# The output gate of a gated linear attention made by seven block products after the heads instead of eight tiles between them

## The chip, the core and the metric

The kernel runs on one core of a Trainium2 chip. The core has five engines with an instruction queue each: TensorE (PE in the profile) for matmuls, VectorE (DVE), ScalarE (ACT), GpSimd (POOL) and SyncE (SP), which here only issues transfers. POOL issues transfers too, and those it issues may add to what lies at their destination. The engines wait for each other by semaphores. What is measured is the time of one execution in microseconds (us); lower is better.

## The reference, cut to what matters

One layer of a decoder trunk, 512 tokens of 1024 channels in fp32:

```python
u = _rmsnorm(h, norm1_g[l])
proj = u @ w_in[l]
a_glu, q, k, v, r, g_low, gate_a, gate_b = _split_cols(proj)

c = a_glu[..., :CONV_CH] * jax.nn.sigmoid(a_glu[..., CONV_CH:])
c = _causal_dwconv(c, conv_dw_w[l], conv_dw_b[l])
c = jax.nn.silu(_layernorm(c, conv_ln_g[l], conv_ln_b[l]))
y_conv = c @ w_conv_out[l]
...
o = _gla_chunked(qh, kh, vh, gkh)
o = o * lax.rsqrt(jnp.mean(o * o, axis=-1, keepdims=True) + EPS) * gla_norm_g[l].astype(jnp.float32)
o = o.reshape(bsz, seq, GLA_VDIM).astype(x.dtype) * jax.nn.silu(r)
y_gla = o @ w_gla_out[l]

merged = jax.nn.sigmoid(gate_a) * y_conv + jax.nn.sigmoid(gate_b) * y_gla
h = h + merged @ w_o[l]
```

After this come an RMSNorm, a channel mixer of width 2816 with a short causal convolution, its residual, and the last RMSNorm. The change concerns r, a 512 x 1024 product of u with a 1024 x 1024 weight.

## The kernel before, in words

**Products in fp32.** Each fp32 operand is split into a high part in a short format and a low part, the rest. A product is three matmuls (`mm3`, lines 448 to 450: low by high, high by low, high by high). Activations are split once; weights are split as they come, in `split_weight`: the high part by an ACT copy (line 385, or 355 for the blocks of summed products), the low part by a DVE subtraction (390, 356). For tiles named in the set `ADDED` the low part is made without DVE: ACT writes the negated weight, rounded to the short format (387), and a transfer issued by POOL adds the weight from memory to it (388).

**A tile** of an ordinary projection is one weight tile of 128 x 1024 (128 output channels, eight blocks of 128 input channels), times all 512 tokens: 8 x 3 = 24 matmuls with 512 columns. The result has channels on partitions.

**Order.** The list `order` gives all weights in the order of use. `weight(...)` takes the next and splits those up to two ahead (`LOOK`), so that DVE, ACT and POOL prepare a weight while PE multiplies an earlier one. Loads are issued by SP in the same order, as buffers come free. Behind each weight, `fill` deals out a share of other DVE work: the taps of the depthwise convolution (`conv_chain`, line 788: 31 taps per channel tile, folded to 46 half-width operations and a few sums), and the list `urgent`. A scheduler arranges each engine's instructions by costs that it assumes, with the waits that follow; on the chip each engine runs its list strictly in order.

**Stages.** First half of v; eight pairs of GLU tiles, each of which starts a chain of taps; the low-rank gate; second half of v. Then four heads, one step apart: for a new head the decays, q (one tile), k (one tile), and for the head before it the scores (line 1031 transposes k), the states and the outputs. In each head stand two tiles of r (`gate_r`, line 1096: the product and silu). Behind the last head come four tiles of merge gate B. `gated` transposes o to channels on partitions (1085), multiplies by gain and silu of r (1088) and splits the result. Next, three tiles of w_gla, and the merge: six groups (`pair_7`, `MERGE`) in which two tiles are made by four block products, with halves of w_gla and w_conv tiles behind them (`BEHIND`). These need sums of token blocks of u, made by DVE as `urgent` work (`token_sums_7`, 1137), and their high and low parts (1145, 1150). The layer norm over the convolved channels runs beside this.

**Seven products.** w_o and w_down are multiplied by `seven`, a scheme in the manner of Strassen: both operands are seen as 2 x 2 blocks, and seven products of sums of blocks (`STEPS`: a11, a12, s1, n2, n3, s4, a22) replace eight. Each product is 24 matmuls of 128x512 for a matrix of this size. The sums of weight blocks are made by accumulating transfers (300, 317) and by DVE (310) in buffers called `kept`; results are added to the residual (1419).

Of the kernel before, what the change touches and what calls it, by code (L numbers as in the profile page):

```python
# [17 lines left out]
P = 128  # L18
D = 1024
T = 512  # L20
# [17 lines left out]
_HALVES = [("w_gla", 3 + h // 2, h % 2) for h in range(10)]  # L38
BEHIND = [_HALVES[:3], _HALVES[3:6], _HALVES[6:9], _HALVES[9:]]
# [4 lines left out]
ADDED = {("w_glu", 2 * k) for k in range(2, KT)} | {("w_r", m) for m in range(KT)}  # L44
ADDED |= {("w_v", KT // 2 + j) for j in (0, 1)}
# [6 lines left out]
SEVEN = {"w_o": KT // 2, "w_down": FT // 2}  # L52
# [23 lines left out]
def trunk_layer(ctx: ExitStack, tc: tile.TileContext, a: dict, out: bass.AP):  # L76
# [135 lines left out]
    order += [("w_glu", 2 * k + j) for k in range(KT) for j in (1, 0)]  # L212
    order += [("w_low", 0), ("w_low", 1)]
    order += [("w_v", KT // 2 + j) for j in range(KT // 2)]
    for h in range(HEADS):
        order += [("w_qk", 2 * h), ("w_qk", 2 * h + 1), ("w_r", 2 * h), ("w_r", 2 * h + 1)]
    order += [("w_gb", m) for m in range(AHEAD)] + [("w_gla", m) for m in range(AHEAD - 1)]
    tight = set()
    first = len(order)
    for (name, p, q), behind in zip(MERGE, BEHIND):  # L220
        for n, part in enumerate(("x1", "x3", "x2", "x4")):
            order.append(("two", (name, p, q, part)))
            order += [tile[:2] for tile in behind[n : n + 1] if tile[2] == 0]
    tight |= set(range(first, len(order)))
# [46 lines left out]
    def block(name, pairs, d, row, col):  # L271

        pairs = pairs[2 * d : 2 * d + 2]
        first = pairs[0][row]
        w = a[name][col * SEVEN[name] + first // 2]
        return w if len(pairs) == 2 else w[:, row * T : (row + 1) * T]

    def keep_tile(name):
        if name == "w_o":
            return tp.tile([P, D], F32, tag="x", name=nm("kept"), bufs=3)  # L280
        return fp.tile([P, D], F32, tag="kept", name=nm("kept"), bufs=2)

    LOADS = {"a11": (0, 0), "a12": (1, 0), "n2": (1, 1), "n3": (0, 1)}

    def load_block(name, pairs, step, d):
# [4 lines left out]
        n = src.shape[-1]  # L290
# [5 lines left out]
        load_dma = nc.sync.dma_start(dst, src)  # L296
        if name == "w_down":
            tc.keep_in_program_order(load_dma)
        if step == "n3":
            nc.gpsimd.dma_start(dst, block(name, pairs, d, 1, 1), accum_op=ALU.add)  # L300
# [12 lines left out]
    def sum_on(name, pairs, step, d):  # L313

        if step in ("a11", "n2"):
            nxt = block(name, pairs, d, *((0, 1) if step == "a11" else (1, 0)))
            nc.gpsimd.dma_start(kept[pairs, d], nxt, accum_op=ALU.add)
# [90 lines left out]
    def weight(name, j, ahead=LOOK):  # L408
# [4 lines left out]
        share = {"two": 2.5, "w_glu": RATE + 0.75}.get(name, RATE)  # L413
# [7 lines left out]
    after, urgent, hold = [], [], [True]  # L421
    behind = []

    def start_chain():
        if not chains and after and not (hold and len(after) == 1):
            chains.append(after.pop()())
# [389 lines left out]
    for k in range(KT):  # L816
        pg = col_tile(weight("w_glu", 2 * k + 1), acts1)
        sg = tmp()
        nc.scalar.activation(sg, pg, AF.Sigmoid)
        pa = col_tile(weight("w_glu", 2 * k), acts1)  # L820
        c = heap()
        nc.vector.tensor_tensor(parted(c), paired(pa), paired(sg), ALU.mult)
        chains.append(conv_chain(k, c))


    ca = [None] * KT
    stat = {}
# [54 lines left out]
    def ln_out(k):  # L882
# [6 lines left out]
        hi = late.tile([P, T], F32R, tag="ch", name=nm("ch"), bufs=KT)  # L889
# [91 lines left out]
    class Head:  # L981
# [79 lines left out]
        def outputs(self):  # L1061
            self.o = tp.tile([P, NT, DV], F32, tag="x", name=nm("o"), bufs=3)
# [15 lines left out]
            for p, half in enumerate(halves):  # L1078
                nc.scalar.activation(self.o[:, p, :], half, AF.Copy, scale=r[:, p : p + 1])

        def gated(self, last=False):
            for s in range(2):
                po = ax_bank() if s or last else mm_bank()
                for p in range(NT):
                    nc.tensor.transpose(po[:, p * P : (p + 1) * P], self.o[:, p, s * P : (s + 1) * P], ident)  # L1085
                f = tmp()
                m = 2 * self.h + s
                nc.vector.scalar_tensor_tensor(f, po, pp[:, PP_GG + s : PP_GG + s + 1], sr[m], ALU.mult, ALU.mult)
                oa[m] = split(f)

    sr = [None] * KT

    def gate_r(m):
        pr = col_tile(weight("w_r", m), acts1)
        sr[m] = heap()
        nc.scalar.activation(sr[m], pr, AF.Silu)
# [118 lines left out]
    def quarters(pool, tag, bufs, halves=1, dt=F32R):  # L1215
# [4 lines left out]
    x_src, x_room, gain_room = quarters(tp, "x", 3, dt=F32), quarters(tp, "x", 3), quarters(tp, "gain", 1)  # L1220
    b_src = quarters(tp, "tmp", 6, 2, F32)
    late_room = lambda: quarters(late, "sums", 3)()
# [3 lines left out]
        {"s1": x_src, "n2": x_src, "s4": b_src, "n3": b_src},  # L1226
        {"s1": c_room, "n2": x_room, "s4": late_room, "n3": late_room},
        {"s1": gain_room, "n2": x_room, "s4": late_room, "n3": x_room},
    )


    heads = [Head(h) for h in range(HEADS)]
    for h in range(HEADS + 1):
        old = heads[h - 1] if h else None
        new = heads[h] if h < HEADS else None
        if new:
            new.decays()
# [3 lines left out]
        if old:  # L1241
            old.scores(heads[h - 2].gated if h > 1 else None)
# [8 lines left out]
    behind += [roots_at[0], low_at[0]]  # L1251
    gla_scope.close()
    late_scope, late = scoped("late", 1, "right")


    s1_n2, of_s1, s4, of_n2, of_s4, n3, of_n3 = merge_sums
    while len(after) > 1:
        fill(1)
    hold.clear()
    start_chain()  # L1260
    chains[0].pop(0)[1]()
    urgent += s1_n2 + of_s1 + s4 + of_n2 + of_s4 + n3 + of_n3
# [28 lines left out]
    for m in range(AHEAD):  # L1291
        part[m] = sigmoid(m, gbs.pop(m))
        if m < AHEAD - 1:
            tile_of("w_gla", m, range(KT))
# [5 lines left out]
    def pair_7(n):  # L1300
        (name, p, q), behind = MERGE[n], BEHIND[n]
        unit = two_tiles(name, p, q, lambda: merge_acts, mm_bank, len(behind) < 3)
        if behind[0][0] == "w_conv":
# [22 lines left out]

    for n in range(4):
        pair_7(n)

# [37 lines left out]
    behind.clear()  # L1367
    late_scope.close()
    res_scope, rp = scoped("residual", 1, "right")
    ctx.push(res_scope)  # L1370


    def seven(name, pairs, acts, complete, at=lambda step, i: None, fine=False):

        bank = {"x": [mm_bank(), mm_bank()], "y": [mm_bank(), mm_bank()], "z": [ax_bank(), ax_bank()]}  # L1380
        of = {"a11": "x", "n2": "x", "n3": "x", "a22": "x", "s1": "y", "s4": "y", "a12": "z"}

        into = {
            "a11": (0, 0, ALU.add, False),
            "a12": (0, 0, ALU.add, True),
            "s1": (1, 1, ALU.add, False),
            "n2": (0, 1, ALU.subtract, False),
            "s4": (0, 1, ALU.add, True),
            "n3": (1, 1, ALU.subtract, True),
            "a22": (1, 0, ALU.add, True),  # L1390
        }

        def products(step, i, parts, acc, lo=0, hi=T, opens=False):
            acc = acc[:, lo:hi]
            opens = opens or step in ("a11", "s1", "a12")
            for d, w in parts:
                for j, pair in enumerate(acts[2 * d : 2 * d + 2]):
                    ah, al = (x[:, i * P : (i + 1) * P] for x in pair[step])
                    c = slice(j * T + lo, j * T + hi)

                    read = 2 * d + j == len(acts) - 1
                    mm3(acc, (ah, al), (w[0][:, c], w[1][:, c]), opens and d == 0 and j == 0, read, not opens)

        steps = list(STEPS)
        while steps:
            step, d = steps.pop(0)

            with tc.issue_after(freed.ins) if step == "a22" and not fine else ExitStack():
                parts = [(d, weight(name, (pairs, step, d)))]
                if steps and steps[0] == (step, 1):  # L1410
                    steps.pop(0)
                    parts.append((1, weight(name, (pairs, step, 1))))
            half, n, op, whole = into[step]
            for i in range(2):
                t = 2 * half + i
                acc = bank[of[step]][i]

                def add(n, acc, c=slice(0, T)):
                    done = nc.vector.tensor_tensor(hres[t, n][:, c], hres[t, n][:, c], acc[:, c], op)  # L1419
                    if whole:  # L1420
                        complete(t, n, c)
                    return done

                if fine and (step, i) == ("a22", 1):
                    products(step, i, parts, acc, 0, H)
                    rest = mm_bank()
                    products(step, i, parts, rest, H, T, True)
                    with tc.manual_schedule(engines={ET.DVE, ET.Activation}):
                        add(n, acc, slice(0, H))
                        add(n, rest, slice(H, T))  # L1430
                    continue
                products(step, i, parts, acc)
                if parts[-1][0] == 1:
                    at(step, i)
                    done = add(n, acc)
                    if (step, i) == ("n3", 1):
                        freed = done
                if fine and (step, i) == ("n3", 1):

# [339 lines left out]
```

## Time and profile before

| | |
|---|---|
| three runs | 821.64, 821.17, 821.0 us; median 821.17 |
| the profiled execution | 820.78 us, its span 818.9 us |
| PE busy | 810.3 us, 99% of the span |
| DVE busy | 715.6 us, 87% |
| ACT busy | 448.9 us, 55% |
| POOL busy | 148.8 us, 18% |
| granted clock of PE | 0.999 of full speed |

The span runs from the first to the last instruction. Busy time counts the instructions on an engine; a matmul's record overlaps with the next one's, so PE's busy time is not the sum of its records' lengths. In a row of groups stand line, engine, operation, output and input tiles, shape and count, then busy time, mean ns of one, and the idle time ahead with what ended it. A row of windows has the stretch, its length, and for PE, weight load, DVE, ACT and POOL the busy time and count, then the granted clock, the share of the 16 DMA engines and GB/s. The waits name who waited for whom: us in total, times, longest. A row of the timeline has start, duration and the instruction. A row of transfers has the count, KB each and the median time from issue to landing.

### The profile page before, as it was taken

The numbers are of one execution on the slowest core, as the hardware profiler recorded it, in microseconds if no ns is written. First come the engines' busy times: TensorE is split into PE (matmuls) and PEld (weight loads), VectorE is DVE, ScalarE is ACT, GpSimd is POOL, SyncE is SP. The second block draws the span as 40 slices with busy tenths as digits, with TensorE's granted clock in tenths as the row PEclk, the third lists the DMA queues.
The fourth block names the chain that finished last, engine by engine and source line by source line (L and its number), as shares of the span: only waits on it lengthen the run. The fifth ranks groups of instructions, "written<-read, shape, count | busy, mean of one in ns | idle before, by whom it ended". The sixth has DMA issues, their size and how long they took to land.

```text
span 818.9 us, 11480 instructions
## 1 busy us (share of the span) xinstructions
PE 810.3 (99%) x4287; PEld 700.5 (86%) x4287; DVE 715.6 (87%) x1157; ACT 448.9 (55%) x666; POOL 148.8 (18%) x133
## 2 busy tenths in 40 slices
PE   9999999999999999999999999999999999999996
PEld 7888888888888889999988898898889988899885
DVE  6689999999989699885788889979965999789896
ACT  6643447656663446684444556556435663466554
POOL 2000010001000213633001000230123301622012
PEclk9999999999999999999999999999999999999999
DMA  8355572563532123223657623146642447334662
GB/s 318 104 127 144 148 188 96 130 154 104 120 97 96 49 62 109 88 78 129 206 115 220 187 71 103 52 161 166 134 137 89 144 123 167 104 103 177 158 129 102
DMA packets 30615, 106.25 MB, mean 130 GB/s; under 512 B 3464, under 2 KB 3600, under 8 KB 30560
## 3 DMA queue, kind: packets, MB, share of 16 engines
q1 hardware_dynamic: 24784, 85.34, 30.4%
q0 software_dynamic: 5760, 20.19, 14.4%
q8 instruction: 33, 0.54, 0.3%
q14 instruction: 22, 0.18, 0.1%
q10 hardware_dynamic: 16, 0.00, 0.0%
HBM read 103.42 MB, written 2.10 MB: 129 GB/s over the span
## 4 chain that ended last, share of the span: by engine, by line
PE 98%; DMA 1%; ACT 0%; DVE 0%; POOL 0%; issue 0%; POOLq 0%; SPq 0%; ACTq 0%
PE mm L448 28%; PE mm L449 28%; PE mm L450 28%; PE mm L662 3%; PE ax L450 2%; PE ax L448 2%; PE ax L449 2%; PE ax L1070 1%; PE ax L1072 1%; PE ax L1051 1%; DMA raw<-in_w_v_dram 1%; PE ax L1040 0%; PE ax L529 0%; PE ax L576 0%; PE ax L1085 0%; PE mm L933 0%
## 5 line engine op out<-in xcount | busy, mean ns | idle before, releaser
L448 PE MATMUL mm<-uh,wlo 128*128 128x512 f32 (+1 forms) x672 | 244.4, 364 | 0.0
L449 PE MATMUL mm<-ul,whi 128*128 128x512 f32 (+1 forms) x672 | 242.4, 361 | 0.0
L450 PE MATMUL mm<-uh,whi 128*128 128x512 f32 (+1 forms) x672 | 242.0, 360 | 0.0
L450 PEld LDWEIGHTS mm<-uh,whi 128*128 128x128 f32 x672 | 126.8, 189 | 19.4
L448 PEld LDWEIGHTS mm<-uh,wlo 128*128 128x128 f32 x672 | 127.0, 189 | 18.8
L449 PEld LDWEIGHTS mm<-ul,whi 128*128 128x128 f32 x672 | 127.0, 189 | 18.6
L385 ACT CAST whi<-raw 128x1024 fp32r<-128x1024 f32 x86 | 89.7, 1047 | 54.9 <-PE mm L450 28.2
L356 DVE TENSOR_TENSOR wlo<-raw,whi 128x1024 fp32r<-128x1024 f32 x80 | 93.1, 1171 | 24.4 <-ACT whi L355 20.5
L327 POOL TENSOR_TENSOR raw<-raw,raw 128x512 f32<-128x512 f32 x42 | 67.6, 1610 | 212.8 <-DVE wlo L356 130.7
L390 DVE TENSOR_TENSOR wlo<-raw,whi 128x1024 fp32r<-128x1024 f32 x70 | 92.7, 1327 | 14.1 <-ACT whi L385 14.0
L355 ACT CAST whi<-raw 128x1024 fp32r<-128x1024 f32 x80 | 76.3, 957 | 34.8 <-PE mm L450 27.2
L788 DVE SCALAR_TENSOR_TENSOR c<-h,pp,c 128x255 f32<-128x255 f32 (+14 forms) x120 | 57.5, 479 | 4.0 <-ACT c L784 3.7
L788 DVE SCALAR_TENSOR_TENSOR c<-aside,btmp,c 128x255 f32<-128x255 f32 (+14 forms) x120 | 57.5, 479 | 1.4 <-ACT c L784 1.4
L788 DVE SCALAR_TENSOR_TENSOR aside<-h,pp,aside 128x255 f32<-128x255 f32 (+6 forms) x112 | 53.7, 479 | 0.0
L355 ACT CAST whi<-kept 128x1024 fp32r<-128x1024 f32 (+1 forms) x32 | 31.8, 996 | 31.8 <-DVE kept L310 17.0
L1503 DVE SCALAR_TENSOR_TENSOR tmp<-mm,pp,tmp 128x511 f32<-128x511 f32 (+1 forms) x56 | 41.4, 742 | 4.0 <-ACT tmp L1500 3.9
L356 DVE TENSOR_TENSOR wlo<-kept,whi 128x1024 fp32r<-128x1024 f32 (+1 forms) x32 | 36.8, 1153 | 4.8 <-ACT whi L355 4.7
L1181 ACT COPY tmp<-mm 128x256 f32<-128x256 f32 x48 | 17.7, 368 | 34.4 <-PE mm L450 34.0
L1419 DVE TENSOR_TENSOR hres<-hres,mm 128x512 f32<-128x512 f32 (+1 forms) x49 | 32.3, 671 | 4.7 <-PE mm L450 3.4
L1500 ACT ACTIVATE tmp<-mm,pp 128x512 f32<-128x512 f32 x28 | 21.8, 779 | 19.0 <-PE mm L450 18.9
L387 ACT ACTIVATE wlo<-raw 128x1024 fp32r<-128x1024 f32 x16 | 16.9, 1060 | 22.1 <-PE mm L448 22.1
L1503 DVE SCALAR_TENSOR_TENSOR tmp<-tmp,pp,tmp 128x511 f32<-128x511 f32 (+1 forms) x32 | 27.8, 887 | 0.4
(347 smaller groups left out, 1767.0 us busy)
## 6 DMA issues: line engine op xcount, KB each, us to landing
raw<-in_w_up_dram SPq DMA_DIRECT2D x44, 512.0 KB, 3.5
raw<-in_w_glu_dram SPq DMA_DIRECT2D x16, 512.0 KB, 5.2
raw<-in_w_down_dram SPq DMA_DIRECT2D x15, 512.0 KB, 4.3
kept<-in_w_down_dram POOLq DMA_DIRECT2D x10, 512.0 KB, 5.9
raw<-in_w_v_dram SPq DMA_DIRECT2D x8, 512.0 KB, 5.6
raw<-in_w_qk_dram SPq DMA_DIRECT2D x8, 512.0 KB, 3.4
raw<-in_w_r_dram SPq DMA_DIRECT2D x8, 512.0 KB, 4.6
wlo<-in_w_r_dram POOLq DMA_DIRECT2D x8, 512.0 KB, 8.1
```

Source lines behind the costliest of these rows:

```text
L327: work = nc.gpsimd.tensor_tensor(out, x, y, ALU.add)
L355: nc.scalar.copy(hi, raw)
L356: two_low[:] = [nc.vector.tensor_tensor(lo, raw, hi.bitcast(F32), ALU.subtract)]
L385: nc.scalar.copy(hi, raw)
L390: pace[0] = nc.vector.tensor_tensor(lo, raw, hi.bitcast(F32), ALU.subtract)
L448: nc.tensor.matmul(acc, ll, rh, start=first, stop=False, **kw)
L449: nc.tensor.matmul(acc, lh, rl, start=False, stop=False, **kw)
L450: nc.tensor.matmul(acc, lh, rh, start=False, stop=last, **kw)
L662: nc.tensor.matmul(acc, act, ready[k // 2][wi][:, j], start=first, stop=last)
L788: nc.vector.scalar_tensor_tensor(out[:, j:], x[:, : half_t - j], w, out[:, j:], ALU.mult, ALU.add)
L1419: done = nc.vector.tensor_tensor(hres[t, n][:, c], hres[t, n][:, c], acc[:, c], op)
L1503: nc.vector.scalar_tensor_tensor(z[:, s:], acc[:, : T - s], w[j], z[:, s:], ALU.mult, ALU.add)
```

## The change

1. The eight r tiles leave the heads. r is made behind the four gate B tiles by `seven("w_r", ...)`, with tokens on partitions (row tiles). The sums of token blocks that merge gate products use serve it too; the first are made during gate B, the rest while r's products run (`sums_for`).
2. Eight loads by SP read the blocks of w_r, each from four tiles in pieces of 1 KB per partition, and sums of blocks are made by twelve accumulating POOL transfers, each of half a block (`add_dram`), and by DVE.
3. The attention output stays with tokens on partitions (`ot`), is multiplied by silu of r there (`put_r`), and is transposed, scaled by the gain and split afterwards (`gated_o`): four tiles at r's last product, four in the first merge group.
4. The last three of the eight GLU pairs move into heads 1 to 3, where the r tiles stood (`LATE_GLU`). Head 0 gets none.
5. Low parts by accumulating transfer: before 16 tiles (6 of w_glu, 8 of w_r, 2 of w_v), after 28 (12 of w_glu, 8 of w_qk, 4 of w_v, 4 of w_gb).
6. Two w_gla tiles follow the first merge group instead of three ahead of it; the other w_gla tiles' halves are spread over the next three groups. The conv norms start in the first merge group.

By the two programs' lists, matmuls of 128x512 go from 2680 to 2656, DVE instructions from 1159 to 1164, ACT instructions from 632 to 656, and transfers issued by POOL of 128x1024 from 37 to 49, with 12 of half that size added; SP issues 178 in both.

```diff
+R_PAIRS = ((0, 4), (1, 5), (2, 6), (3, 7))
+LATE_GLU = 3
-_HALVES = [("w_gla", 3 + h // 2, h % 2) for h in range(10)]
-BEHIND = [_HALVES[:3], _HALVES[3:6], _HALVES[6:9], _HALVES[9:]]
+_HALVES = [("w_gla", 2 + h // 2, h % 2) for h in range(12)]
+BEHIND = [[], _HALVES[:4], _HALVES[4:8], _HALVES[8:]]
...
-ADDED = {("w_glu", 2 * k) for k in range(2, KT)} | {("w_r", m) for m in range(KT)}
-ADDED |= {("w_v", KT // 2 + j) for j in (0, 1)}
+ADDED = {("w_glu", j) for j in range(4, 2 * KT)} | {("w_qk", m) for m in range(KT)}
+ADDED |= {("w_v", KT // 2 + j) for j in range(KT // 2)} | {("w_gb", m) for m in range(AHEAD)}
...
-        order += [("w_qk", 2 * h), ("w_qk", 2 * h + 1), ("w_r", 2 * h), ("w_r", 2 * h + 1)]
-    order += [("w_gb", m) for m in range(AHEAD)] + [("w_gla", m) for m in range(AHEAD - 1)]
+        order += [("w_qk", 2 * h), ("w_qk", 2 * h + 1)]
+        if h:
+            order += glu_order[KT - LATE_GLU + h - 1]
+    order += [("w_gb", m) for m in range(AHEAD)]
+    order += [("w_r", (R_PAIRS, step, d)) for step, d in STEPS]
...
+    def add_dram(name, t, src):
+        t = shaped(name, t)
+        for part in (slice(0, 2), slice(2, 4)) if name == "w_r" else (slice(None),):
+            nc.gpsimd.dma_start(t[:, part], src[:, part], accum_op=ALU.add)
...
-        share = {"two": 2.5, "w_glu": RATE + 0.75}.get(name, RATE)
+        share = {"two": 2.5, "w_glu": RATE + 0.75, "w_r": 2.0}.get(name, RATE)
...
+    def gated_o(m, bank):
+        po = bank()
+        c = (m % 4) * P
+        for p in range(NT):
+            nc.tensor.transpose(po[:, p * P : (p + 1) * P], ot[p, m // 4][:, c : c + P], ident)
+        gain = pp[:, PP_GG + m % 2 : PP_GG + m % 2 + 1]
...
+        nc.scalar.activation(hi, po, AF.Copy, scale=gain)
+        low_at[:] = [nc.vector.scalar_tensor_tensor(lo, po, gain, hi.bitcast(F32), ALU.mult, ALU.subtract)]
+        oa[m] = hi, lo
...
         if new:
+            late_glu = glu(KT - LATE_GLU + h - 1)
             new.decays()
             new.queries()
         else:
             gate_b(0)
         if old:
-            old.scores(heads[h - 2].gated if h > 1 else None)
+            old.scores()
+        if not new:
+            urgent += s1_n2[:3] + of_s1
         new.keys() if new else gate_b(1)
         if old:
             old.states()
-        gate_r(2 * h) if new else gate_b(2)
-        if old:
+            next(late_glu) if new else gate_b(2)
             old.outputs()
-        gate_r(2 * h + 1) if new else gate_b(3)
-    heads[-1].gated(True)
+            next(late_glu) if new else gate_b(3)
...
+    def put_r(step, t, n, acc):
+        if step in ("a11", "s1", "n2"):
+            rt[t, n] = rp_.tile([P, T], F32, tag="r", name=nm("r"), bufs=8)
+            return nc.scalar.copy(rt[t, n], acc)
+        if step == "a22":
+            rt[t, n] = rp_.tile([P, T], F32, tag="r", name=nm("r"), bufs=8)
+            nc.scalar.activation(rt[t, n], acc, AF.Silu)
+        else:
+            r = rt[t, n]
+            one, two = (r, acc) if step == "n3" else (acc, r)
+            done = nc.vector.tensor_tensor(r, one, two, ALU.add if step == "a12" else ALU.subtract)
+            nc.scalar.activation(r, r, AF.Silu)
+        nc.vector.tensor_tensor(ot[t, n], ot[t, n], rt[t, n], ALU.mult)
+        return done if step == "n3" else None
+
+    def r_at(step, i):
+        if (step, i) == ("a22", 1):
+            for m in range(4, KT):
+                gated_o(m, ax_bank)
+
+    seven("w_r", R_PAIRS, [ByTile(k) for k in range(4)], None, r_at, put=put_r, before=sums_for)
...
+            if n == 0 and j in (1, 2):
+                for m in range(2 * j - 2, 2 * j):
+                    gated_o(m, ax_bank)
+                if j == 2:
+                    start_norms()
```

More of the change, by code (lines that the diff above doesn't have):

```diff
@@ L51 @@
 ET = mybir.EngineType
-SEVEN = {"w_o": KT // 2, "w_down": FT // 2}
+SEVEN = {"w_o": KT // 2, "w_down": FT // 2, "w_r": KT // 2}
 STEPS = [("a11", 0), ("a11", 1), ("a12", 0), ("s1", 0), ("a12", 1), ("s1", 1)]
@@ L223, in trunk_layer @@
             order += [tile[:2] for tile in behind[n : n + 1] if tile[2] == 0]
+        if not behind:
+            order += [("w_gla", 0), ("w_gla", 1)]
     tight |= set(range(first, len(order)))
@@ L814, in trunk_layer, with glu @@
     sum_taps()
-    for k in range(KT):
+    def glu(k):
         pg = col_tile(weight("w_glu", 2 * k + 1), acts1)
@@ L823, in trunk_layer @@
         chains.append(conv_chain(k, c))
+        conv_given.append(1)
+        yield
+    for k in range(KT - LATE_GLU):
+        list(glu(k))
     ca = [None] * KT
+    chp = None
     stat = {}
@@ L1078, in outputs @@
             for p, half in enumerate(halves):
[L1079 to L1096, printed above, removed]
+                if self.h % 2 == 0:
+                    ot[p, self.h // 2] = heap()
+                c = slice((self.h % 2) * DV, (self.h % 2 + 1) * DV)
+                nc.scalar.activation(ot[p, self.h // 2][:, c], half, AF.Copy, scale=r[:, p : p + 1])
+    ot = {}
+    def gated_o(m, bank):
[4 more added lines that the diff above has]
+        gain = pp[:, PP_GG + m % 2 : PP_GG + m % 2 + 1]
+        if m < 3:
+            both = tp.tile([P, 2, T], F32R, tag="x", name=nm("oa"), bufs=3)
+        elif m == 3:
+            both = tp.tile([P, 2, T], F32R, tag="gain", name=nm("oa"), bufs=1)
+        hi, lo = (both[:, 0, :], both[:, 1, :]) if m < 4 else (heap(F32R), heap(F32R))
+        nc.scalar.activation(hi, po, AF.Copy, scale=gain)
+        low_at[:] = [nc.vector.scalar_tensor_tensor(lo, po, gain, hi.bitcast(F32), ALU.mult, ALU.subtract)]
+        oa[m] = hi, lo
     gbs = {}
@@ L1302, in pair_7 @@
         unit = two_tiles(name, p, q, lambda: merge_acts, mm_bank, len(behind) < 3)
-        if behind[0][0] == "w_conv":
+        if behind and behind[0][0] == "w_conv":
             while chains:
@@ L1370, in trunk_layer @@
     ctx.push(res_scope)
[L1373 to L1438, printed above, removed]
-                    c = slice(H, T)
-                    nc.vector.tensor_tensor(hres[t, 0][:, c], hres[t, 0][:, c], acc[:, c], ALU.add)
```

131 lines of the change are left out of this document (107 added, 24 removed).

## The prediction

> **What bounds the kernel now.** I read the page's busy table and chain first, then the waits of PE, then PE's pace, and last the busy time of each engine by stage.
>
> ```profile
> span 818.9 us, 11480 instructions
> PE 810.3 (99%) x4287; PEld 700.5 (86%) x4287; DVE 715.6 (87%) x1157; ACT 448.9 (55%) x666; POOL 148.8 (18%) x133
> PEclk9999999999999999999999999999999999999999
> PE 98%; DMA 1%; ACT 0%; DVE 0%; POOL 0%; issue 0%; POOLq 0%; SPq 0%; ACTq 0%
> ```
> ```profile
> PE mm L568 <- DVE ones L541: 1.1, 1, 1.1
> PE mm L662 <- ACT h L589: 0.8, 1, 0.8
> ```
> ```profile
> 40.02 0.39 PE L450 MATMUL mm<-uh,whi 128*128 128x512 f32 x1
> ...
> 41.38 0.39 PE L450 MATMUL mm<-uh,whi 128*128 128x512 f32 x1
> ```
> ```profile
> 33.00:149.00 116.00, 116.00 (x513) 96.11 (x512) 108.07 (x242) 59.53 (x81) 9.41 (x11) 1.00 0.55 147
> 149.00:260.00 111.00, 111.00 (x527) 93.35 (x527) 106.06 (x243) 62.68 (x104) 9.72 (x9) 1.00 0.47 121
> 260.00:400.00 140.00, 140.00 (x852) 125.85 (x851) 116.70 (x154) 80.60 (x128) 42.27 (x26) 1.00 0.27 91
> 418.00:457.00 39.00, 39.00 (x174) 32.31 (x173) 31.99 (x45) 17.50 (x24) 5.17 (x6) 1.00 0.76 188
> ```
>
> TensorE carries 98% of the chain and waits twice, for 1.9 us in all, at the very start. Its clock is granted in full. Six steps of the timeline take 41.38 − 40.02 = 1.36 us: a 128x512 matmul costs 0.2267 us from start to start, and its record of 0.39 overlaps the next. So each matmul taken away is worth 0.227 us, as long as nothing new makes PE wait. The windows say how near that is. In the GLU stage (33 to 149) and in the heads (149 to 260) VectorE is busy 108 of 116 and 106 of 111 us; in the merge (260 to 400) 117 of 140; in the stage of w_o (418 to 457), which already uses the seven-product scheme, 32 of 39.
>
> **The change, part by part.** (1) Fewer products. The eight r tiles are 8×8×3 = 192 matmuls of 128x512; seven products of 24 are 168. PE saves 24 × 0.2267 = **−5.44 us**. The tile transposes of o stay, as do all other matmuls, in new places.
>
> (2) The low parts. The helper that makes a weight's low half has two ways:
>
> ```profile
> L385 ACT CAST whi<-raw 128x1024 fp32r<-128x1024 f32 x86 | 89.7, 1047 | 54.9 <-PE mm L450 28.2
> L390 DVE TENSOR_TENSOR wlo<-raw,whi 128x1024 fp32r<-128x1024 f32 x70 | 92.7, 1327 | 14.1 <-ACT whi L385 14.0
> L387 ACT ACTIVATE wlo<-raw 128x1024 fp32r<-128x1024 f32 x16 | 16.9, 1060 | 22.1 <-PE mm L448 22.1
> L388 POOL DMA_DIRECT2D wlo<-in_w_r_dram x8 | 7.0, 877 | 97.8 <-ACT junk L1074 32.3 <-DVE c L788 30.2 <-ACT wlo L387 28.5
> ```
>
> Tiles made by the accumulating DMA rise from 16 to 28 (the 8 of r go, 20 others come: 6 glu, 8 qk, 2 v, 4 gb). Against those 20 made by subtraction DVE is spared 20 × 1.33 = 27 us, and ACT gets 20 × 1.06 = 21 us. ACT is busy 62.7 of 111 us in the heads, so that lies beside PE. What the spared DVE time buys is the new DVE work of (4).
>
> (3) The heads. Where two r tiles stood in each head, heads 1 to 3 now get a pair of glu tiles, as long on PE (2 × 24 × 0.2267 = 10.9 us). Head 0 gets nothing: between the last matmul of its keys and the transposes of k (line 1031) there remains one qk tile, 24 × 0.2267 = 5.44 us. Here is that stretch now:
>
> ```profile
> 156.75 0.39 PE L450 MATMUL mm<-uh,whi 128*128 128x512 f32 x1
> 173.30 0.49 PE L1031 MATMUL ax<-ident,k 128*128 128x128 f32 x3
> ```
> ```profile
> 157.09 0.48 DVE L788 SCALAR_TENSOR_TENSOR c<-h,pp,c 128x246 f32<-128x246 f32 x1
> ...
> 160.94 0.47 DVE L788 SCALAR_TENSOR_TENSOR c<-aside,btmp,c 128x243 f32<-128x243 f32 x1
> 161.33 0.69 DVE L1021 TENSOR_TENSOR k<-mm,tmp 128x512 f32<-128x512 f32 x1
> ...
> 162.26 0.35 DVE L1025 TENSOR_TENSOR k<-k,tmp 128x192 f32<-128x192 f32 x1
> ```
>
> k is ready at 162.61, that is 5.86 us after the last keys matmul began, and wanted only at 173.30. In that time DVE ran 11 taps, (160.94 − 157.09)/10 = 0.385 us each, and 1.28 us on k. By the program's order only four of the 11 are listed behind that matmul, so DVE was 7 taps, 2.7 us, behind its place. The new order lists eight. If DVE is in its place, k is ready at 0.34 + 8 × 0.385 + 1.28 = 4.7 us and PE, which comes after 5.44 + 0.23 = 5.67, doesn't wait; if it is 7 taps behind, at 7.4 us, and PE waits 1.7. Bounds 0 and 1.7; I take **+1.2**, nearer the late end, since DVE has 5 us of slack in 111.
>
> (4) The r stage: 168 matmuls, 38.1 us of PE. DVE's list in it: 13 low parts of 128x1024 and 2 sums of kept tiles; 14 halves of token sums, 6 low parts of sums, 6 additions of products, 6 multiplications with o (all 32 of 128x512); 3 taps. Nearest rows:
>
> ```profile
> L356 DVE TENSOR_TENSOR wlo<-kept,whi 128x1024 fp32r<-128x1024 f32 x28 | 34.2, 1220 | 4.8 <-ACT whi L355 4.7
> L1419 DVE TENSOR_TENSOR hres<-hres,mm 128x512 f32<-128x512 f32 x47 | 31.4, 681 | 4.7 <-PE mm L450 3.4 <-DMA hres<-in_x_dram 1.2
> ```
>
> By records 15 × 1.22 + 32 × 0.681 + 3 × 0.48 = 41.5 us. Records of neighbours overlap by about 0.09 us (0.48 against 0.385 for taps): 50 × 0.09 less is 37.0. The list is as long as the stage, where w_o's stage has 32 of 39. Bounds: no wait, since DVE work at the stage's end is wanted only behind it, and 41.5 − 38.1 = 3.4. I take **+1.0**, a bit under the middle, as the list's end (low parts for the next stage) can run on. ACT has 14 high parts there (1.05 each, 14.7 us) and some 20 smaller operations, which fit into 38 us.
>
> (5) After r, the first w_gla tiles follow one merge group instead of coming ahead of it. They need o's high and low parts; the last of these and the start of the conv norms are queued on DVE with the tiles' own low parts. Bounds 0 (the same tile waits for nothing now) and 1.5 (one 1.22 us low part ahead of it in the queue, less or more a tap); I take the middle, **+0.8**.
>
> (6) Transfers. Rows of their landing now:
>
> ```profile
> raw<-in_w_r_dram SPq DMA_DIRECT2D x8, 512.0 KB, 4.6
> wlo<-in_w_r_dram POOLq DMA_DIRECT2D x8, 512.0 KB, 8.1
> wlo<-in_w_glu_dram POOLq DMA_DIRECT2D x6, 512.0 KB, 7.6
> DMA to landing us min/median/max: 5.4/8.0/10.7
> ```
>
> In the new order the low parts by DMA are issued 15 to 20 us of PE time before use (one qk tile: 10.0), against a median landing of 8.0 and a longest of 10.7. The r blocks' adds have 12 to 22 us, but the kept block of the last product's second half only 8.2 to its cast. A block is now read in runs of 1 KB; no row shows these. I cost the transfers at nothing, covered by those leads; without cover, 10.7 − 8.2 + 0.88 for the second half's issue = 3.4 us at that block. SP's queue gets 8 loads where it had 8, the first two early; POOL's gets 24 more issues of 0.88 us, 21 us in all, on an engine busy 9.7 of 111 us. Behind an issue that waits for ACT's negated copy stand only further issues and four small rstd steps of the heads, which I also cost at nothing; a rstd late by an issue is 0.9 us, with products of the next head for cover.
>
> [...]
>
> Sum: −5.44 + 1.2 + 1.0 + 0.8 = −2.44 us. The profiled execution took 820.78 us (its span 818.9 and 1.9 around it), so 818.34; it lies 0.39 under the median of the three runs, 821.17. On the median that is **818.7**.
>
> **The rivals.** A is this forecast: a bit under half of the gain arrives.
>
> B: no new wait, the whole gain arrives: 821.17 − 5.44 = 815.7. For it: the DVE time spared in the heads is 27 us, its lag could be gone before head 0 ends, and the w_o stage runs the same scheme without a wait. Against it: the taps fill what is spared, since they are dealt out by matmuls passed.
>
> C: VectorE becomes the bound in the r stage, and the change costs time. The list of 41.5 us by records against 38.1 of PE gives 3.4; the lag that DVE brings along (2.7 us in the heads now) adds to it, since nothing in the stage lets it catch up: 6.1, with 1.2 at head 0: 7.3 against 5.44, so 821.17 + 1.9 = 823.0. It turns slower once DVE's list takes over 38.1 + 2.7 us, lag included. For it: no stage before has a list as long as its PE time. Against: w_o's 32 of 39, and gate_b's tiles ahead of r, whose low parts come from the DMA now, give DVE room to catch up.
> [...]
>
> D: the adds by DMA land late. If the 1 KB runs, or two to three times as many POOL DMAs in flight, bring landings to about 12 us, the kept block waits 12 − 8.2 + 0.9 = 4.7, and the qk tile with its lead of 10.0 another 2.0; with head 0's 1.2 (DVE catches up in the new waits, so the others of A go): −5.44 + 7.9 = +2.5: 823.7. For it: landings of POOL adds already reach 10.7. Against: the DMA share of 0.47 in the heads, and all leads but these two are 12 us or more.
>
> **How the numbers follow.** A change under 0.2% (1.64 us) can't be told from none here: faster is below 819.5, slower above 822.8. A has 0.44, B 0.17, C 0.26, D 0.13. A's own range is 817 to 820.5: 0.30 of its 0.44 is faster, 0.14 the same; B is faster; C runs from 820 to 825, 0.11 of its 0.26 the same; D is slower. Together faster 0.47, same 0.25, slower 0.28. The range from 815.9 to 823.8 takes in most of B and of C, and leaves out 0.2.
>
> **What would show it.** PE's count of 128x512 matmuls down by 24. In PE's waits: line 1057 (the transposes of k) on DVE's k, about 1 us, at head 0 alone; a wait of PE in the r stage on DVE's low parts or token sums, below 2 us (C: over 4); w_gla's first tile on a low part. A window over the r stage with DVE near its whole length. Landings of the w_r adds under 10 us (D: 12 or more, with ACT's cast of the kept block waiting for a DMA). It is wrong if PE waits elsewhere: at late glu tiles whose bank or low part is not free, or at the conv norms, which now start later with less time until w_conv.

## The result and the profile after

The changed kernel takes 841.64 us (median of four runs, 841.28 to 845.09) against 821.38 us for the kernel before, measured beside it: 1.0256 times as long, 95% interval 1.0229 to 1.0284. The forecast was 818.7 us, range 815.9 to 823.8. The profiled execution of the changed kernel took 841.78 us, its span 840.0.

From the page after: the span, the busy engines, PE's share and granted clock in 40 slices of 21 us, and the chain that ended last.

```profile
span 840.0 us, 11519 instructions
PE 809.8 (96%) x4263; PEld 698.1 (83%) x4263; DVE 713.6 (85%) x1162; ACT 467.9 (56%) x690; POOL 171.1 (20%) x157
PE   9999999999998498999999999999999999999996
PEclk9999999999999699999999999999999999999999
PE 74%; DVE 17%; issue 3%; ACT 2%; POOL 2%; DMA 1%; POOLq 0%; SPq 0%; DVEq 0%; ACTq 0%
```

And PE's waits after:

```profile
PE mm L467 <- DVE r L1420: 14.4, 1, 14.4
PE ax L889 <- ACT sum L920: 3.2, 1, 3.2
PE ax L1057 <- DVE k L1051: 1.8, 1, 1.8
PE mm L587 <- DVE ones L560: 1.1, 1, 1.1
PE mm L467 <- ACT oa L1122: 1.0, 1, 1.0
PE mm L467 <- ACT whi L374: 0.9, 1, 0.9
```

PE's part of the chain falls from 98% to 74%. The span grows by 21.1 us, although 24 matmuls (5.4 us) are gone, so 26.5 us are to be found. Five new waits make 14.4 + 3.2 + 1.8 + 1.0 + 0.9 = 21.3. About three more go to stretches in which PE was granted half its clock. Windows of PE behind the two longest waits (length, then busy time and count of PE, weight load, DVE, ACT and POOL; the number after them is the clock):

```profile
286.00:288.00 2.00, 2.00 (x6) 1.61 (x5) 2.00 (x4) 0.97 (x2) 0.00 (x0) 0.50 0.04 8
288.00:290.00 2.00, 2.00 (x10) 1.56 (x10) 2.00 (x4) 0.54 (x1) 0.00 (x0) 0.98 0.00 0
...
322.00:326.00 4.00, 4.00 (x21) 3.86 (x21) 2.82 (x4) 0.99 (x2) 0.00 (x0) 0.57 0.53 177
```

Behind the first wait, matmuls of 128x512 come 0.43 us apart for some 3 us (six in 2 us instead of nine): seven of them lose 0.2 us each, 1.4 us. Behind the second, matmuls of 128x256 come 0.21 us apart instead of 0.12, and a clock of 0.57 over 4 us loses (1 − 0.57) × 4 = 1.7 us. The last 2 us were not traced. The runs below show half clock behind waits of 1.9 us (noadd, 0.55) and 3.0 us (ring2048, 0.50) too, and a clock of 1.00 behind a wait of 2.5 us in combo and one of 3.2 us in ring2048.

Why PE waits 14.4 us is seen on POOL. Its timeline after, each row one half-block sum of w_r, with the idle time ahead of it and what ended that:

```profile
220.78 1.20 POOL L300 DMA_DIRECT2D kept<-in_w_r_dram  x1 [7.32 <-DVE c L807]
225.56 1.21 POOL L300 DMA_DIRECT2D kept<-in_w_r_dram  x1 [3.58 <-issue]
230.22 1.18 POOL L300 DMA_DIRECT2D kept<-in_w_r_dram  x1 [3.46 <-DVE c L807]
...
275.72 1.21 POOL L300 DMA_DIRECT2D kept<-in_w_r_dram  x1 [3.40 <-issue]
```

ACT's row for the weight that waits for the last of these, and PE's first matmul behind it:

```profile
280.21 1.04 ACT L374 CAST whi<-kept 128x1024 fp32r<-128x1024 f32 x1 [8.27 <-DMA kept<-in_w_r_dram]
```
```profile
284.99 0.76 PE L467 MATMUL mm<-whi,ul 128*128 128x512 f32 x1 [14.45 <-DVE r L1420]
```

Twelve issues start 4.6 to 6.8 us apart, of which 1.2 us is the issue and mostly some 3.4 us idle time. Seven of the eleven gaps have no releaser ("issue"); the other four name an engine, and their issues are no closer. From the first to the last it is 275.72 − 220.78 = 54.9 us, where r's products are 38.1 us of PE. The last sum lands at 280; the high part follows, the low part, and then, behind the low part in DVE's queue, the reading of a PSUM bank (L1420) that PE's next product writes. Landing itself is quick: 4.4 us in the median, 6.5 at the longest.

### The profile page after: what moved, and what is told of

Its sections match the earlier page's. It is cut to its first block, busy times and chain, and to the rows that moved or that the text cites. A ratio compares the mean times of both kernels' runs of the same rounds, so it can differ in the third digit from the quotient of the medians.

```text
span 840.0 us, 11519 instructions
## 1 busy us (share of the span) xinstructions
PE 809.8 (96%) x4263; PEld 698.1 (83%) x4263; DVE 713.6 (85%) x1162; ACT 467.9 (56%) x690; POOL 171.1 (20%) x157
## 4 chain that ended last, share of the span: by engine, by line
PE 74%; DVE 17%; issue 3%; ACT 2%; POOL 2%; DMA 1%; POOLq 0%; SPq 0%; DVEq 0%; ACTq 0%
PE mm L467 21%; PE mm L468 21%; PE mm L469 21%; DVE c L807 6%; DVE aside L807 3%; PE mm L681 3%; PE ax L469 2%; PE ax L467 2%; PE ax L468 2%; DVE wlo L375 2%; POOL raw L346 1%; DMA raw<-in_w_v_dram 1%; DMA kept<-in_w_r_dram 1%; DVE h L842 0%; PE ax L1077 0%
## 5 line engine op out<-in xcount | busy, mean ns | idle before, releaser
L467 PE MATMUL mm<-uh,wlo 128*128 128x512 f32 (+1 forms) x608 | 220.1, 362 | 0.0
L468 PE MATMUL mm<-ul,whi 128*128 128x512 f32 (+1 forms) x608 | 218.1, 359 | 0.0
L469 PE MATMUL mm<-uh,whi 128*128 128x512 f32 (+1 forms) x608 | 217.8, 358 | 0.0
L469 PEld LDWEIGHTS mm<-uh,whi 128*128 128x128 f32 x608 | 115.4, 190 | 17.0
L467 PEld LDWEIGHTS mm<-uh,wlo 128*128 128x128 f32 x608 | 115.6, 190 | 16.6
L468 PEld LDWEIGHTS mm<-ul,whi 128*128 128x128 f32 x608 | 115.5, 190 | 16.3
L375 DVE TENSOR_TENSOR wlo<-raw,whi 128x1024 fp32r<-128x1024 f32 x86 | 100.2, 1171 | 33.6 <-ACT whi L374 29.8
L409 DVE TENSOR_TENSOR wlo<-raw,whi 128x1024 fp32r<-128x1024 f32 x50 | 66.6, 1335 | 7.5 <-ACT whi L404 7.3
L375 DVE TENSOR_TENSOR wlo<-kept,whi 128x1024 fp32r<-128x1024 f32 (+1 forms) x40 | 46.5, 1165 | 16.5 <-ACT whi L374 16.4
L406 ACT ACTIVATE wlo<-raw 128x1024 fp32r<-128x1024 f32 x28 | 29.6, 1060 | 49.1 <-PE mm L467 40.4
L467 PE MATMUL mm<-whi,ul 128*128 128x512 f32 x48 | 19.5, 406 | 14.4 <-DVE r L1420 14.4
```

What stands on the lines that cost most here:

```text
L375: two_low[:] = [nc.vector.tensor_tensor(lo, raw, hi.bitcast(F32), ALU.subtract)]
L406: pace[0] = nc.scalar.mul(lo, raw, -1.0)
L409: pace[0] = nc.vector.tensor_tensor(lo, raw, hi.bitcast(F32), ALU.subtract)
L467: nc.tensor.matmul(acc, ll, rh, start=first, stop=False, **kw)
L468: nc.tensor.matmul(acc, lh, rl, start=False, stop=False, **kw)
L469: nc.tensor.matmul(acc, lh, rh, start=False, stop=last, **kw)
```

## Experiments

**1. The sums of w_r's blocks.** Four kernels start from the changed one. The first leaves the sums out, the second has a `dynamic_dma_scratch_size` of 2048 instead of 1024 bytes in the program's head (the expectations say bytes for descriptors), the others use other forms of the same transfers.

```diff
 noadd:
-        t = shaped(name, t)
-        for part in (slice(0, 2), slice(2, 4)) if name == "w_r" else (slice(None),):
-            nc.gpsimd.dma_start(t[:, part], src[:, part], accum_op=ALU.add)
+        if name != "w_r":
+            nc.gpsimd.dma_start(t, src, accum_op=ALU.add)
 ring2048:
-    ... dynamic_dma_scratch_size=1024)
+    ... dynamic_dma_scratch_size=2048)
 rows4k:
+        nc.gpsimd.dma_start(t, a[name][0] if name == "w_r" else src, accum_op=ALU.add)
```

In forms each of the six block sums takes another form of the call; the expectation names them. My own case in all four was that a transfer of 256 rows holds up the next one while the setting is 1024, and one of 128 rows much less: 824.5 us for noadd, ring2048 and rows4k, and a wait before the last r product of less than 8 us in forms. Against it stood, for ring2048, a distance of 4.65 us at either setting, with 841 us, or transfers that land late, after 8 us and more, with 835 us or more; for forms, a distance that goes by bytes or by the length of a run.

> The twelve accumulating transfers that sum blocks of w_r are left out (so r is wrong); all else of the changed kernel stays. Theory (POOL's issues of these transfers are what is late: one half block each 4.65 us, 1.2 of them shown and 3.4 idle before the next): PE's waits of 14.4 us before the last r product and of 0.9 us at its second product go, and so does the slower stretch of matmuls behind the long wait (about 1.5 us); waits at k (1.8), at the conv norm's sums (3.2) and at o's split (1.0) stay: 841.6 - 17 = about 824.5 us. Rival (VectorE's list in the r stage is the bound, and the transfers only fill the time): at least half of the 14.4 us stays as a wait on DVE, 833 or more.

> [...]

> The six block adds take six forms (r is wrong, since some add another part of the weight): the first in quarters of 128 rows of 1 KB; the second in halves of 128 rows of 2 KB; the third in halves of 256 rows of 2 KB from two tiles; the fourth in halves of 256 rows of 1 KB, all from one tile; the fifth as in the changed kernel, halves of 256 rows of 1 KB from two tiles; the sixth whole, 128 rows of 4 KB. [...]

> Each block add reads 512 KB in rows of 4 KB from one weight tile in one transfer, instead of two halves in 1 KB runs from four tiles (r is wrong; as many bytes are added). [...] Rival (the added bytes, 6.3 MB read again in this stage, are what is late): landings of 8 us and a wait of 8 us or more stay.

Measured: noadd 829.52, ring2048 830.57 (828.31 to 831.76; 1.009 of the kernel before, 1.0065 to 1.0115), rows4k 830.29, forms 837.12 us. The kernel before took 822.19 us beside them, 0.8 more than beside the changed kernel; noadd, rows4k and forms are single runs, and the first two lie within ring2048's spread. In forms PE still waits 9.0 us, where I had expected less than 8. POOL in ring2048, two halves to a row:

```profile
223.41 2.44 POOL L300 DMA_DIRECT2D kept<-in_w_r_dram  x2 [7.42 <-DVE c L807]
229.43 2.40 POOL L300 DMA_DIRECT2D kept<-in_w_r_dram  x2 [3.58 <-DVE state L1084]
```

And in forms, where the first two rows are the quarters and the last two are halves of 256 rows of 2 KB:

```profile
223.19 2.62 POOL L303 DMA_DIRECT2D kept<-in_w_r_dram  x3 [7.26 <-DVE c L829]
226.63 0.87 POOL L303 DMA_DIRECT2D kept<-in_w_r_dram  x1 [0.82 <-issue]
...
238.37 1.14 POOL L303 DMA_DIRECT2D raw<-in_w_r_dram  x1 [0.67 <-DMA raw<-in_w_r_dram]
243.01 1.10 POOL L303 DMA_DIRECT2D raw<-in_w_r_dram  x1 [3.49 <-issue]
```

With 2048 bytes two halves go out 1.2 us apart, and they land after 5.6 us in the median, not the 8 us and more of the rival; at 1024 bytes 256 rows of 2 KB stand 4.6 us apart just like 256 rows of 1 KB, while 128 rows go out three in a row and then pause. rows4k adds as many bytes and has no such wait (2.9 us before the last product). So neither the bytes nor the length of a run sets the distance here. Two things moved it: the setting (4.65 us apart at 1024 bytes, 1.2 at 2048) and the rows of a transfer (at 1024, one of 256 rows or three of 128 before a pause). The gain of 11.1 us from the setting is nearly that of leaving the sums out (12.1). At 1024 bytes the next transfer of 256 rows is issued about when the one before has landed: that is my estimate from the distance of 4.65 us being about a landing (4.4). What the bytes are used for, and what holds the next transfer back, no run shows.

A way round at 1024 bytes is to cut the transfers smaller:

```diff
 quarters:
-        for part in (slice(0, 2), slice(2, 4)) if name == "w_r" else (slice(None),):
+        for part in (0, 1, 2, 3) if name == "w_r" else (slice(None),):
```

> The changed kernel with its 1024 bytes for descriptors, each block of w_r added in four transfers of 128 rows of 1 KB instead of two of 256 rows. [...] Rival (POOL needs 4.6 us for 256 rows however they are cut): 2.3 us each, 56 us in all, and 841 us again.

Measured: 831.59 us, where I had expected the 830.6 of ring2048. The first four quarters go out from 223.0 to 227.3. Twelve more issues, and 10.05 us less than the changed kernel (841.64): the rival's 841 us did not come. That the time is so near that of ring2048 is in part chance: here PE waits 4.1 us before the last product, still for a transfer (ACT waits 5.0 us for the last quarter), and in ring2048 3.0 us for another reason.

My 824.5 us for noadd, ring2048 and rows4k was 5 to 6 us too low. I had counted every wait in the r stage as one of the transfers, and half clock with them. What is left, in ring2048, besides 0.9 us for a high part:

```profile
PE ax L889 <- ACT sum L920: 3.2, 1, 3.2
PE mm L467 <- DVE r L1420: 3.0, 1, 3.0
```

**2. POOL's additions against VectorE.** DVE in ring2048, two multiplications (1.28 us for the pair where POOL adds nothing) and a low part (1.22), and POOL's additions of weight pairs, at 267 for the first merge group and at 300 for the second, all from SBUF to SBUF:

```profile
254.37 1.28 DVE L1422 TENSOR_TENSOR h<-h,r 128x512 f32<-128x512 f32 x2
...
267.80 3.49 DVE L1422 TENSOR_TENSOR h<-h,r 128x512 f32<-128x512 f32 x2
271.21 2.28 DVE L375 TENSOR_TENSOR wlo<-kept,whi 128x1024 fp32r<-128x1024 f32 x1
```
```profile
267.47 3.26 POOL L346 TENSOR_TENSOR raw<-raw,raw 128x512 f32<-128x512 f32 x2 [7.25 <-DMA raw<-in_w_gb_dram]
270.70 1.71 POOL L346 TENSOR_TENSOR raw<-raw 128x512 f32<-128x512 f32 x1
...
300.25 6.72 POOL L346 TENSOR_TENSOR raw<-raw,raw 128x512 f32<-128x512 f32 x2 [19.23 <-DVE wlo L409]
```

DVE's three operations take 3.3 us too long, 1.1 us each, beside three POOL additions on end (3.26 and 1.71 us). At 300 it is the other way: POOL's pair, 3.26 us at 267, takes 6.72 while DVE's operations there keep their length. ACT's high part then waits 4.1 us for the sum, and DVE, whose queue holds the norm's sums behind the low part, 2.3 us for that high part:

```profile
307.00 1.05 ACT L374 CAST whi<-raw 128x1024 fp32r<-128x1024 f32 x1 [4.10 <-POOL raw L346]
```

The kernel before has the first group's additions where DVE is idle for 4.7 us, and they cost nothing there. Its next addition does show the effect, 3.41 us at 299.79 where one alone takes 1.3, and no wait of PE came of it:

```profile
277.09 2.64 POOL L327 TENSOR_TENSOR raw<-raw,raw 128x512 f32<-128x512 f32 x2
...
299.79 3.41 POOL L327 TENSOR_TENSOR raw<-raw,raw 128x512 f32<-128x512 f32 x1 [18.81 <-DVE wlo L356]
```
```profile
280.68 1.41 DVE L1088 SCALAR_TENSOR_TENSOR tmp<-ax,pp,h 128x512 f32<-128x512 f32 x2 [4.66 <-PE ax L1085]
```

The experiment leaves these additions out. I had expected the two waits of 3.0 and 3.2 us to fall below 0.5 us each, with 1.6 us of half clock behind each gone as well, and 821.5 us; against it stood a VectorE whose list by itself is too long in both places, with both waits above 2 us and 828 us or more.

```diff
 nosums (on ring2048):
+            if (name, p) in (("w_gb", 4), ("w_gb", 6)):
+                nc.sync.dma_start(three, a[name][p])
+                return
             add(three[:, left], one[:, left], two[:, left])
...
```

> The kernel with 2048 bytes for descriptors, without the sums that POOL makes of weight pairs for the first two merge groups (line 346; the tile of sums is loaded from memory by SP instead, so these tiles' gates are wrong). [...]

Measured: 821.08 us. PE's waits that remain:

```profile
PE ax L1061 <- DVE k L1055: 1.8, 1, 1.8
PE mm L471 <- ACT oa L1126: 0.9, 1, 0.9
PE mm L471 <- ACT whi L378: 0.8, 1, 0.8
```

Both waits of 3 us are gone, and with them the half clock, which in ring2048 stood behind the first in the first two rows (14 matmuls that lose 0.2 us each, 2.8 us) and not behind the second, in the last row:

```profile
276.00:278.00 2.00, 2.00 (x6) 1.54 (x5) 2.00 (x5) 0.21 (x1) 0.00 (x0) 0.50 0.04 8
278.00:280.00 2.00, 2.00 (x6) 1.52 (x6) 2.00 (x4) 0.28 (x1) 0.36 (x1) 0.50 0.00 0
...
312.00:314.00 2.00, 1.71 (x12) 1.62 (x13) 1.66 (x3) 1.41 (x3) 0.00 (x0) 1.00 0.76 262
```

Instead of 1.6 us of half clock behind each wait, 2.8 and none make nearly the same sum, so that the total came out so well is luck.

Leaving the additions out takes away POOL's work and the wait for its results at once; what separates a disturbance between the two engines from a mere lack of DVE time are the lengthened operations above (1.1 us on each of DVE's three, 6.72 us instead of 3.26 for POOL's pair), and that the wait of 3.2 us at the norm is gone in combo and early too, where DVE makes the same additions itself. By what means one engine's operations lengthen the other's, no run shows.

**3. Head 0 and the end of the r stage.** Two single edits on ring2048:

```diff
 glu4:
-LATE_GLU = 3
+LATE_GLU = 4
-        if h:
-            order += glu_order[KT - LATE_GLU + h - 1]
+        order += glu_order[KT - LATE_GLU + h]
...
 actput:
+            if step == "n3":
+                out = tmp()
+                freed = nc.scalar.copy(out, acc)
+                acc = out
...
```

> The kernel with 2048 bytes for descriptors and a fourth pair of GLU tiles moved, into head 0, so that each head has two tiles in r's place. Theory (head 0's k has too little cover): the wait of 1.8 us at the transposes of k goes and none comes in its place: 828.6 us. Rival (VectorE's lag only moves on): a wait of like size comes in a later head or the waits behind r grow, 830 us or more.

> The kernel with 2048 bytes for descriptors, in which the fifth of r's results in time (n3) is copied out of PSUM by ScalarE first and subtracted by VectorE from the copy, so that PE's next product into the same bank waits for ScalarE and not for VectorE's queue. Theory (VectorE comes late to r's last results, since its list is held up by POOL's sums just before): the wait of 3.0 us falls to about 1 us, now on a low part, and with it the stretch at half clock: 830.6 - 3.5 = 827 us. Rival (the wait is for the low parts anyway): the wait stays at 2.5 us or more, 830 us.

Measured: 831.66 and 831.52 us, single runs, both within ring2048's spread. In glu4 the wait for k is gone, as expected, and so is that before the last r product (here POOL's pair is the one held up, 5.73 us), but 2.8 us stand at the transposes of o (behind DVE's low parts of o) and 0.8 at a q or k tile's transfer: its rival was right, the lateness moves on. In actput the wait before the last product falls from 3.0 to 1.0 us, as expected, but 2.5 us come at the transposes of o, and the wait for a high part grows from 0.9 to 2.5: the time is the rival's, by other waits than it named.

**4. All together.** Four kernels on ring2048, in which DVE makes the additions that disturb it, in its own order, and the first two w_gla tiles are multiplied in the order 4 to 7, 0 to 3 of their blocks (`SWAP`). combo has the edits of glu4 and actput as well. combo_early is combo with the second set of token sums dealt out during gate B, combo_noact is combo_early without actput, and early is combo_early without glu4 and actput.

```diff
 all four:
+            engine = nc.vector if (name, p) in (("w_gb", 4), ("w_gb", 6)) else nc.gpsimd
+            work = engine.tensor_tensor(out, x, y, ALU.add)
...
-                tile_of("w_gla", m, range(KT))
+                tile_of("w_gla", m, SWAP)
 early, combo_early, combo_noact:
-            urgent += s1_n2[:3] + of_s1
+            urgent += s1_n2[:3] + of_s1 + s1_n2[3:] + of_n2
...
-    urgent += s1_n2[3:] + of_n2 + s4 + of_s4 + n3 + of_n3
+    urgent += s4 + of_s4 + n3 + of_n3
```

In combo I had expected the waits at k, at the norm's sums and at o's split gone, 1 us left before the last r product, and 819 us.

> 2048 bytes for descriptors, GLU pair in head 0, n3's result copied out by ScalarE, the sums of the first two merge groups made by VectorE instead of POOL, and the first two w_gla tiles multiplied in the order 4 to 7, 0 to 3 of their blocks, so that the last transposed tiles of o are wanted last. [...] Rival (VectorE is the bound of the r stage and the first merge groups): the sums it now makes itself add 8 x 0.6 = 5 us to its list, and the time stays above 824 us.

> The changed kernel with 2048 bytes for descriptors, the first two merge groups' sums on VectorE, the block order 4 to 7, 0 to 3 in the first w_gla tiles, and the second set of token sums (n2) dealt out during gate B, ahead of taps, instead of at the start of the r stage; head 0 and n3's result as in the change. Theory (VectorE's list in the r stage is a matter of order: taps that nobody waits for stand ahead of sums that PE waits for): the wait for n2's weights (0.9 us) goes, k's wait of 1.8 stays, and with the sums off POOL the waits before the last r product and at the norm go: 821.2 - 5.4 + 2 + 2 (VectorE's lag in the last product) = about 819.5 us. Rival (the taps put off come back as a wait at the norms): a wait of 2 us or more there, 822 or more.

> The kernel of combo (823.4 us) with the n2 token sums dealt out during gate B. Theory: its wait of 2.5 us for the high part of n2's second block, which stands in ScalarE's queue behind silus that wait for VectorE, falls below 1 us; that for a q or k tile's transfer (1.2) stays: 823.4 - 2 = 821.4 us. Rival (the wait is of ScalarE's own order): it stays, 823 us or more.

> The same without the copy of n3's result by ScalarE. Theory (that copy and the second wait for high parts go together, since it was 0.9 us without and 2.5 us with it): no wait over 1.2 us is left but at the last r product, where 1 us or less stays as POOL is out of the way: 820.5 us. Rival (VectorE is late at the last product by its own list): 3 us there, 823 us.

Measured, each as a ratio to the kernel before on the same chip: combo 823.37 us, 1.0025 (1.0014 to 1.0036); early 828.23, 1.0072 (1.0055 to 1.0089); combo_early 825.11, 1.0036 (1.0023 to 1.0049); combo_noact 827.81, 1.0067 (1.0045 to 1.009). All four came out slower than expected, and none beats the kernel before. combo's new waits:

```profile
PE mm L468 <- ACT whi L375: 2.5, 1, 2.5
PE mm L468 <- DMA wlo<-in_w_qk_dram: 1.2, 1, 1.2
```

early's:

```profile
PE mm L469 <- DVE r L1423: 3.3, 1, 3.3
PE ax L1060 <- DVE k L1054: 1.7, 1, 1.7
PE mm L469 <- DVE wlo L411: 1.5, 1, 1.5
```

In combo_early the wait for the high part is gone, as expected, but the sums dealt out earlier left the r stage's share free, and `fill` gave it to 27 taps between 241 and 275 us (some 10 us; none in combo). PE waits 1.3 us for a low part that stands behind taps and 1.7 at the transposes of o.

In early and combo_noact (11 and 13 taps there) PE waits 3.3 and 3.6 us before the last r product, where the rival of combo_noact had 3, but DVE is not late by its list: it is idle, as is ACT, until the last transfer has landed. POOL, ACT and DVE in early:

```profile
261.11 1.20 POOL L301 DMA_DIRECT2D kept<-in_w_r_dram  x1 [1.67 <-issue]
```
```profile
269.15 1.04 ACT L376 CAST whi<-kept 128x1024 fp32r<-128x1024 f32 x1 [4.27 <-DMA kept<-in_w_r_dram]
```
```profile
270.23 1.23 DVE L377 TENSOR_TENSOR wlo<-kept,whi 128x1024 fp32r<-128x1024 f32 x1 [3.49 <-ACT whi L376]
```

It is issued 2 us later than in ring2048 and lands about 8 us after; why both, was not traced. A share of none for the taps in this stage was not measured. What stays open is whether an order of DVE's work exists that brings r's stage through without a wait; combo comes within 2.4 us of the kernel before (823.37 against 820.98).

## Why the prediction was wrong, by its own steps

Step 1, the saving: 24 matmuls fewer, as forecast; at the pace shown it is still 5.4 us. In nosums, 821.08 us against 820.98 for the kernel before beside it, 3.5 us of it go to the three waits quoted; the other 2 us are in small gaps that were not traced.

Step 2, the low parts by transfer in the heads: no wait in the changed kernel. In glu4 and combo the one tile whose lead I had named as shortest, a q or k tile, waits 0.8 and 1.2 us for its low part.

Step 3, head 0: 1.2 forecast, 1.8 measured, at the place named and in head 0 alone; it is just beyond my bound of 1.7.

Step 4, the r stage: "+1.0". Without the transfers in its way it is 1.9 (noadd) to 3.0 (ring2048), inside the bound of 3.4, but not for the reason given: without POOL's additions it is none (nosums). The list of DVE fits in nosums; what stretches it is POOL's additions beside it (1.1 us on each of three operations in ring2048), of which the sum had nothing. The sum had no half clock either, which comes on top behind these waits (1.6 us in noadd, 2.8 in ring2048).

Step 5, the first w_gla tile: 0.8 forecast, 1.0 measured. The conv norms, named as what would make the forecast wrong, cost 3.2 us, and 1.7 of half clock in the changed kernel, where POOL's pair of additions takes 6.71 us.

Step 6 is the one that failed: "POOL's gets 24 more issues of 0.88 us, 21 us in all" and "I cost the transfers at nothing". I took an issue's length for its cost in the queue. The form of transfer used for r's sums costs 4.65 us from issue to issue, 12 × 4.65 = 56 us in a stage of 38. I had bounded landings (4.4 us after in the median, below all rows that I showed) and said that no row shows 1 KB runs, yet gave no bound for the distance between issues. What came of it is PE's wait of 14.4 us with half clock behind it. The trace before shows the distance for transfers of 128 rows, here three on end:

```profile
683.08 0.87 POOL L300 DMA_DIRECT2D raw<-in_w_down_dram  x1 [6.88 <-DVE hres L1419]
684.29 0.85 POOL L317 DMA_DIRECT2D kept<-in_w_down_dram  x1 [0.33 <-issue]
685.49 0.88 POOL L317 DMA_DIRECT2D kept<-in_w_down_dram  x1 [0.35 <-DVE wlo L356]
```

1.21 us for 128 rows would have made 2.4 for 256 had it gone by rows, 12 × 2.4 = 29 us, still under 38; these rows alone would not have told it. The setting in the program's head, which no step of the prediction looks at, makes the difference: 4.65 us at 1024 bytes, 1.2 at 2048.

The rivals: B did not occur. C, DVE as the bound of the r stage, is what the next 3 us consist of, with another cause. D named the right block (the kept block of the last product) and the right queue, and had the wrong mechanism for the changed kernel, late landing, and a third of the price (4.7 for 14.4); a late landing does make the wait in early and combo_noact. In ring2048 POOL issues two halves in 2.4 us beside a VectorE at work, so the issues themselves were not slow there.

## What to carry to other kernels

For a queue that issues transfers, price the distance from issue to issue (here 4.65 us) and not the length of an issue (1.2), and read it from a run of the new form; here a `dynamic_dma_scratch_size` of 2048 bytes brought the issues to 1.2 us apart, and transfers of 128 rows went out three in a row at 1024. Look at which engine's SBUF-to-SBUF work falls beside which when a stage moves: POOL's additions, free beside an idle VectorE in the kernel before, made three of VectorE's operations 1.1 us longer each in ring2048, or were held up themselves, one from 1.3 to 5.0 us in noadd. And look at the clock behind each new wait of TensorE: in ring2048 one wait of 3.0 us cost 2.8 us more in half clock, another of 3.2 us nothing.

## What the runs showed of the hardware that I had not expected

Transfers of 256 rows issued by POOL stood 4.65 us apart with a `dynamic_dma_scratch_size` of 1024 bytes and 1.2 us with 2048, and 24 transfers of 128 rows were faster than 12 of 256 (831.6 against 841.6 us for the kernel). A small operation on POOL, `rstd` of 128x4, took 1.2 us in one place and 3.2 beside VectorE's additions:

```profile
210.98 1.19 POOL L519 TENSOR_TENSOR rstd<-mean,mhalf 128x4 f32<-128x4 f32 x1 [8.29 <-DVE mean L1101]
...
234.62 3.20 POOL L519 TENSOR_TENSOR rstd<-mean,mhalf 128x4 f32<-128x4 f32 x1 [2.79 <-DVE mean L1101]
```

(both in ring2048). And the granted clock fell to 0.55 behind a wait of 1.9 us in noadd, the first row, and stayed at 1.00 behind one of 2.5 us in combo, the second:

```profile
273.00:275.00 2.00, 1.92 (x5) 1.57 (x6) 1.90 (x3) 2.00 (x3) 0.00 (x0) 0.55 0.01 4
```
```profile
258.00:260.00 2.00, 1.93 (x8) 1.29 (x8) 2.00 (x4) 2.00 (x4) 0.00 (x0) 1.00 1.01 153
```

The same wait of 3.2 us at the conv norm's sums had a clock of 0.57 behind it in the changed kernel and 1.00 in ring2048, so the length of a wait alone does not decide it.
